# Binary cross entropy on one core: how the rows of the second chunk and of the last two stores are dealt to the 16 DMA engines

## The chip, the core and the metric

One core of a Trainium2 chip. The metric is the device time of one execution in microseconds (us). Before the change three runs gave 1864.62, 1865.15 and 1865.41; the median is 1865.15 us.

## The reference

Two float32 arrays of 8192 x 8192 go in, one comes out; target holds 0 or 1.

```python
pred = np.clip(pred, 1e-7, 1 - 1e-7)
return -(target * np.log(pred) + (1 - target) * np.log(1 - pred))
```

Since target is 0 or 1, the result is -ln|target - 1 + pred|, and so the kernel computes it: clip, add target - 1, absolute value, logarithm, times -1.

## The kernel before, in words

**Tiling.** The arrays are taken as flat; 64 Mi elements over 128 partitions are 524288 columns. `plan` (lines 17 to 24) cuts them into chunks: two of `FIRST` = 5120 columns, 35 of `BIG` = 14336, two of `LAST` = 5632 and one of `TAIL` = 1024. A chunk is one contiguous stretch of memory, cut into 128 rows, a row for each partition; a row of a `FIRST` chunk is 20480 bytes, of a `BIG` one 57344, of a `LAST` one 22528, of the `TAIL` one 4096.

**Buffers.** `ring_p` holds prediction chunks in three slots of `BIG` columns and a place for the tail; everything is computed in place there and stored from there. `ring_t` holds one target chunk as bf16; the transfer that loads it converts. The first two chunks share a slot.

**Queues.** Transfers are issued from three queues. ScalarE (ACT) issues the first prediction load as two halves (lines 69 and 70). GpSimd (POOL) issues all other loads (lines 72 and 75) and most stores (line 79). SyncE (SP) issues the stores of the last three chunks (a and b by line 79, c by `store_rows`, line 84). All of them run on the same 16 DMA engines. `store_rows` cuts the last store into 108, 12 and 8 rows. A transfer of fewer than 128 rows need not use all 16 engines: the semaphore records show 12, 12 and 8 landings for these three pieces, where one of 128 rows has 16.

**Compute.** VectorE (DVE) clips (`clip`, line 88), adds target - 1 (`log`, line 94) and multiplies by -1 (`back`, line 102); ScalarE does Abs and Ln between these (lines 97 and 98).

**Order.** It is written out by hand from line 104 on. At the start: both target loads and prediction loads of chunks 0 and 1, then the load of chunk 2; compute on 0 and 1; then the third target load (line 115), which may not be issued before line 94 of chunk 1 has read its target; then the stores of chunks 0 and 1 and the prediction load of chunk 3. In the middle, each chunk has its target load, its store and the prediction load two chunks on, in that order. At the end come chunks a, b (5632 columns each) and c (1024 columns).

Of the kernel before, what the change touches and what calls it, by code (L numbers as in the profile page):

```python
# [1 line left out]

# [4 lines left out]

EPS = 1e-7

BIG = 14 * 1024  # L10
FIRST = 5 * 1024
LAST = 5632
TAIL = 1024
SLOTS = 3


def plan(total):
    n = (total - 2 * FIRST - 2 * LAST - TAIL) // BIG
    assert n > 4 and total == 2 * FIRST + n * BIG + 2 * LAST + TAIL
    spots = [(FIRST, 0, 0), (FIRST, FIRST, FIRST)]  # L20
    spots += [(BIG, k % SLOTS * BIG, 0) for k in range(1, n + 1)]
    end = (n + 1) % SLOTS * BIG
    spots += [(LAST, end, 0), (LAST, end + LAST, LAST)]
    return spots + [(TAIL, SLOTS * BIG, BIG)]


@with_exitstack
def kernel(
    ctx: ExitStack,
    tc: tile.TileContext,  # L30
    pred: bass.AP,
    target: bass.AP,
    out: bass.AP,
):
    nc = tc.nc
    fp32 = mybir.dt.float32
    bf16 = mybir.dt.bfloat16
    Alu = mybir.AluOpType
    Act = mybir.ActivationFunctionType
    P = nc.NUM_PARTITIONS  # L40

    R, C = pred.shape
    spots = plan(R * C // P)
    n = len(spots)
    widths = [s[0] for s in spots]
    cols = [sum(widths[:k]) for k in range(n)]

    def chunk(ap, k):
        flat = ap.rearrange("r c -> (r c)")
        return flat[cols[k] * P : (cols[k] + widths[k]) * P].rearrange("(p w) -> p w", p=P)  # L50

    pool = ctx.enter_context(tc.tile_pool(name="rings", bufs=1))
    ring_p = pool.tile([P, SLOTS * BIG + TAIL], fp32, name="ring_p", tag="ring_p")
    ring_t = pool.tile([P, BIG + TAIL], bf16, name="ring_t", tag="ring_t")
    warm = pool.tile([1, 8], fp32, name="warm", tag="warm")

    def spot(k, part=(0, 1)):
        w, c, _ = spots[k]
        i, m = part
        return ring_p[:, c + i * w // m : c + (i + 1) * w // m]  # L60

    def spot_t(k, part=(0, 1)):
        w, _, c = spots[k]
        i, m = part
        return ring_t[:, c + i * w // m : c + (i + 1) * w // m]

    def load_p(k):
        if k == 0:
            for rows in (slice(0, P, 2), slice(1, P, 2)):
                nc.scalar.dma_start(out=spot(0)[rows], in_=chunk(pred, 0)[rows])  # L70
        else:
            nc.gpsimd.dma_start(out=spot(k), in_=chunk(pred, k))  # L72

    def load_t(k):
        nc.gpsimd.dma_start(out=spot_t(k), in_=chunk(target, k))  # L75

    def store(k):
        queue = nc.sync if k >= n - 3 else nc.gpsimd
        queue.dma_start(out=chunk(out, k), in_=spot(k))  # L79

    def store_rows(k):
        src, dst = spot(k), chunk(out, k)
        for first, last in ((0, 108), (108, 120), (120, 128)):
            nc.sync.dma_start(out=dst[first:last], in_=src[first:last])

    def clip(k, *part):
        p = spot(k, *part)
        nc.vector.tensor_scalar(  # L88
            out=p, in0=p, scalar1=EPS, scalar2=1 - EPS, op0=Alu.max, op1=Alu.min
        )  # L90

    def log(k, *part):
        p = spot(k, *part)
        nc.vector.scalar_tensor_tensor(  # L94
            out=p, in0=spot_t(k, *part), scalar=1.0, in1=p, op0=Alu.subtract, op1=Alu.add
        )
        nc.scalar.activation(out=p, in_=p, func=Act.Abs)  # L97
        nc.scalar.activation(out=p, in_=p, func=Act.Ln)  # L98

    def back(k, *part):  # L100
        p = spot(k, *part)
        nc.vector.tensor_scalar(out=p, in0=p, scalar1=-1.0, scalar2=None, op0=Alu.mult)  # L102

    with tc.manual_schedule():
        nc.vector.memset(warm, 1.0)  # L105
        load_t(0)
        load_p(0)
        load_t(1)
        load_p(1)
        load_p(2)  # L110
        nc.scalar.activation(out=warm, in_=warm, func=Act.Ln)  # L111
        for k in (0, 1):
            clip(k)
            log(k)
        load_t(2)
        back(0)
        store(0)
        back(1)
        store(1)
        load_p(3)  # L120
        a, b, c = range(n - 3, n)
        for k in range(2, n - 3):
            for h in (0, 1):
                clip(k, (h, 2))
                log(k, (h, 2))
            if k < n - 4:
                load_t(k + 1)
            else:
                load_t(a)
                load_t(b)  # L130
                load_p(c)
                load_t(c)
                back(k, (0, 2))
                for j in (a, b):
                    clip(j)
            if k < n - 4:
                back(k, (0, 2))
            back(k, (1, 2))
            store(k)
            if k + 2 < n - 3:  # L140
                load_p(k + 2)
            elif k + 2 == n - 3:
                load_p(a)
                load_p(b)
        log(a, (0, 2))
        log(a, (1, 2))
        clip(c)
        log(b, (0, 2))
        back(a, (0, 2))
        log(b, (1, 2))  # L150
        back(a, (1, 2))
        store(a)
        log(c)
        back(b, (0, 2))
        back(b, (1, 2))
        store(b)
        back(c)
        store_rows(c)


# [1 line left out]
_INS = ['pred', 'target']  # L162
_OUTS = [((8192, 8192), 'float32')]


# [23 lines left out]
```

## Time and profile before

| | |
|---|---|
| span of the profiled execution (first to last instruction) | 1863.3 us |
| runs, median of 3 | 1865.15 us (1864.62 to 1865.41) |
| DVE busy | 1121.6 us (60%) |
| ACT busy | 902.4 us (48%) |
| POOL busy | 178.7 us (10%) |
| prediction loads of 7168 KB, issue to landing, median | 44.3 us |
| target loads of 3584 KB, issue to landing, median | 31.3 us |
| stores of 7168 KB, issue to landing, median | 31.1 us |

The page gives the profiled execution's time as its span alone; the runs' median is 1.85 us more, for what lies ahead of the first instruction and behind the last.

How to read it: the DMA row has the mean busy share of the 16 engines in 40 slices of the span, in tenths. A stretch has the busy time of each compute engine, the granted TensorE clock (not used here), the DMA share and GB/s; a packet is counted where it starts, so a short stretch can show over 1.00. The GB/s count a target at the two bytes an element that are written, not the four that are read. In the order of time, a line has the start, the duration, the engine, the line of the program, the operation and its shape, how many, and in brackets how long the engine sat idle before it and what ended that. Beside these views the trace holds a record for each DMA packet (start, duration, size, queue, but not the engine) and one for each semaphore update (so, for each transfer, a landing for every engine that it used).

### The profile page before, as it was taken

To read this page: it belongs to the slowest core of one execution; us is meant where nothing else is said; L and a number is where in the kernel's file an instruction comes from. 1 tells how busy PE (TensorE), PEld (TensorE's weight loads), DVE (VectorE), ACT (ScalarE), POOL (GpSimd) and SP (SyncE) were. 2 spreads that over 40 slices of the span, in tenths; PEclk is the share of its full clock that TensorE was granted. 3 is DMA by queue.
4 is the path that set the end of the run, shared out by engine and by line. 5 is a ranking of instruction groups with operands and counts; after the bars stand their busy time and mean duration, and the time that the engine had idled before them with its cause. 6 is when DMAs were issued, how large, how long until landed. Compare 5 with 4: busy or idle time off the path is not lost.

```text
span 1863.3 us, 713 instructions
## 1 busy us (share of the span) xinstructions
DVE 1121.6 (60%) x230; ACT 902.4 (48%) x156; POOL 178.7 (10%) x120
## 2 busy tenths in 40 slices
DVE  4666555555666566655555666566655555666565
ACT  4454444455555544444445555544444445555554
POOL 1111101111110011101111110011101111110020
DMA  9999999999999999999999999999999999999999
GB/s 344 348 370 356 355 356 355 355 355 355 357 375 374 374 372 355 355 355 355 355 355 355 359 374 374 375 375 361 355 355 356 356 356 355 356 367 374 374 353 352
DMA packets 17318, 671.15 MB, mean 360 GB/s; under 512 B 1952, under 2 KB 1952, under 8 KB 2336
## 3 DMA queue, kind: packets, MB, share of 16 engines
q0 software_dynamic: 16704, 662.18, 99.0%
q1 hardware_dynamic: 448, 6.29, 0.8%
q10 hardware_dynamic: 160, 2.62, 0.4%
q14 instruction: 6, 0.05, 0.0%
HBM read 536.87 MB, written 268.44 MB: 432 GB/s over the span
## 4 chain that ended last, share of the span: by engine, by line
DMA 60%; issue 35%; ACT 3%; DVE 1%; POOL 0%; POOLq 0%; DVEq 0%; PEldq 0%
DMA ring_t<-in_target_dram 58%; DMA ring_p<-in_pred_dram 2%; ACT ring_p L98 1%; ACT ring_p L97 1%; DVE ring_p L94 1%; DVE ring_p L102 0%; POOL out_dram L79 0%; DVE ring_p L88 0%; POOL ring_t L75 0%; POOLq L75 0%; POOL ring_p L72 0%; POOLq L79 0%; DVEq L94 0%; PEldq L184 0%
## 5 line engine op out<-in xcount | busy, mean ns | idle before, releaser
L97 ACT ACTIVATE ring_p<-ring_p 128x7168 f32<-128x7168 f32 (+3 forms) x77 | 452.0, 5870 | 940.7 <-DVE ring_p L94 940.7
L94 DVE SCALAR_TENSOR_TENSOR ring_p<-ring_t,ring_p 128x7168 f32<-128x7168 bf16 (+3 forms) x77 | 558.2, 7251 | 372.0 <-DMA ring_t<-in_target_dram 370.7
L102 DVE TENSOR_SCALAR ring_p<-ring_p 128x7168 f32<-128x7168 f32 (+3 forms) x77 | 285.4, 3707 | 329.4 <-ACT ring_p L98 329.4
L98 ACT ACTIVATE ring_p<-ring_p 128x7168 f32<-128x7168 f32 (+3 forms) x77 | 452.6, 5877 | 2.4
L88 DVE TENSOR_SCALAR ring_p<-ring_p 128x7168 f32<-128x7168 f32 (+3 forms) x75 | 284.6, 3794 | 24.4 <-DMA ring_p<-in_pred_dram 24.4
L79 POOL DMA_DIRECT2D out_dram<-ring_p x37 | 128.0, 3459 | 584.4 <-DVE ring_p L102 584.2
L75 POOL DMA_DIRECT2D ring_t<-in_target_dram x40 | 29.0, 724 | 1057.2 <-DVE ring_p L94 1056.4
L72 POOL DMA_DIRECT2D ring_p<-in_pred_dram x39 | 21.8, 561 | 2.5 <-issue 2.5
L111 ACT ACT_TABLE_LOAD x1 | 1.3, 1283 | 1.9 <-issue 1.9
L105 DVE MEMSET warm<- 1x8 f32 x1 | 0.1, 65 | 0.8 <-PEq L173 0.8
L111 ACT ACTIVATE warm<-warm 1x8 f32<-1x8 f32 x1 | 0.2, 208 | 0.0
L173 POOL MEMSET const-float32-0.0<- 128x1 f32 x1 | 0.1, 99 | 0.2 <-issue 0.2
L173 POOL MEMSET const-bfloat16-1.0<- 128x1 bf16 x1 | 0.1, 102 | 0.0
L173 POOL MEMSET const-uint8-127<- 128x1 uint8 x1 | 0.1, 100 | 0.0
L173 POOL MEMSET const-float32-1.0<- 128x1 f32 x1 | 0.1, 99 | 0.0
## 6 DMA issues: line engine op xcount, KB each, us to landing
ring_p<-in_pred_dram POOLq DMA_DIRECT2D x35, 7168.0 KB, 44.3
out_dram<-ring_p POOLq DMA_DIRECT2D x35, 7168.0 KB, 31.1
ring_t<-in_target_dram POOLq DMA_DIRECT2D x35, 3584.0 KB, 31.3
ring_p<-in_pred_dram POOLq DMA_DIRECT2D x2, 2816.0 KB, 37.1
out_dram<-ring_p SPq DMA_DIRECT2D x2, 2816.0 KB, 14.6
out_dram<-ring_p POOLq DMA_DIRECT2D x2, 2560.0 KB, 27.9
ring_t<-in_target_dram POOLq DMA_DIRECT2D x2, 1408.0 KB, 26.5
ring_p<-in_pred_dram ACTq DMA_DIRECT2D x2, 1280.0 KB, 10.5
```

Source lines behind the costliest of these rows:

```text
L72: nc.gpsimd.dma_start(out=spot(k), in_=chunk(pred, k))
L75: nc.gpsimd.dma_start(out=spot_t(k), in_=chunk(target, k))
L79: queue.dma_start(out=chunk(out, k), in_=spot(k))
L88: nc.vector.tensor_scalar(out=p, in0=p, scalar1=EPS, scalar2=1 - EPS, op0=Alu.max, op1=Alu.min)
L94: nc.vector.scalar_tensor_tensor(out=p, in0=spot_t(k, *part), scalar=1.0, in1=p, op0=Alu.subtract, op1=Alu.add)
L97: nc.scalar.activation(out=p, in_=p, func=Act.Abs)
L98: nc.scalar.activation(out=p, in_=p, func=Act.Ln)
L102: nc.vector.tensor_scalar(out=p, in0=p, scalar1=-1.0, scalar2=None, op0=Alu.mult)
L105: nc.vector.memset(warm, 1.0)
L111: nc.scalar.activation(out=warm, in_=warm, func=Act.Ln)
L173: nc = _bacc.Bacc("TRN2", target_bir_lowering=False, num_devices=1)
```

## The change

The first two chunks become 4096 and 6144 columns. The second chunk's prediction load becomes five transfers: 112 rows; a small read of 8 rows x 16 elements into a new tile `turn` that nothing reads; 8 rows; the small read again; the last 8 rows. The small reads are there to move on the choice of engines, so that the eights fall to engines 8 to 15. The store of chunk b becomes three transfers of 112, 8 and 8 rows, and that of chunk c 48, 72 and 8 rows instead of 108, 12 and 8. What is computed stays the same.

```diff
-FIRST = 5 * 1024
+FIRST = 4 * 1024
+SECOND = 6 * 1024
...
-    n = (total - 2 * FIRST - 2 * LAST - TAIL) // BIG
-    assert n > 4 and total == 2 * FIRST + n * BIG + 2 * LAST + TAIL
-    spots = [(FIRST, 0, 0), (FIRST, FIRST, FIRST)]
+    n = (total - FIRST - SECOND - 2 * LAST - TAIL) // BIG
+    assert n > 4 and total == FIRST + SECOND + n * BIG + 2 * LAST + TAIL
+    spots = [(FIRST, 0, 0), (SECOND, FIRST, FIRST)]
...
+    turn = pool.tile([8, 32], fp32, name="turn", tag="turn")
...
         if k == 0:
             for rows in (slice(0, P, 2), slice(1, P, 2)):
                 nc.scalar.dma_start(out=spot(0)[rows], in_=chunk(pred, 0)[rows])
+        elif k == 1:
+            src, dst = chunk(pred, 1), spot(1)
+            nc.gpsimd.dma_start(out=dst[:112], in_=src[:112])
+            for i in range(2):
+                rows, few = slice(112 + 8 * i, 120 + 8 * i), slice(16 * i, 16 * i + 16)
+                nc.gpsimd.dma_start(out=turn[:, few], in_=src[:8, few])
+                nc.gpsimd.dma_start(out=dst[rows], in_=src[rows])
         else:
             nc.gpsimd.dma_start(out=spot(k), in_=chunk(pred, k))
...
-    def store_rows(k):
+    def store_rows(k, *ends):
         src, dst = spot(k), chunk(out, k)
-        for first, last in ((0, 108), (108, 120), (120, 128)):
+        for first, last in zip((0, *ends), (*ends, P)):
             nc.sync.dma_start(out=dst[first:last], in_=src[first:last])
...
-        store(b)
+        store_rows(b, 112, 120)
         back(c)
-        store_rows(c)
+        store_rows(c, 48, 120)
```

## The prediction

> **What bounds the kernel now.** I read the page first, then stretches of the span, then the order of time at both ends, then SyncE's waits.
>
> ```profile
> span 1863.3 us, 713 instructions
> ...
> DVE 1121.6 (60%) x230; ACT 902.4 (48%) x156; POOL 178.7 (10%) x120
> ...
> DMA  9999999999999999999999999999999999999999
> ...
> q0 software_dynamic: 16704, 662.18, 99.0%
> q1 hardware_dynamic: 448, 6.29, 0.8%
> ```
>
> No slice of the DMA engines is under 90%, while the busiest compute engine has 40% free. One chunk in the middle, and the last microseconds, as stretches:
>
> ```profile
> 1094.10:1144.84 50.74, 30.64 (x6) 24.60 (x5) 4.68 (x4) 1.00 1.00 362
> ...
> 1859.00:1860.00 1.00, 0.00 (x0) 0.00 (x0) 0.00 (x0) 1.00 0.96 352
> 1860.00:1861.00 1.00, 0.00 (x0) 0.00 (x0) 0.00 (x0) 1.00 0.22 88
> 1861.00:1862.00 1.00, 0.00 (x0) 0.00 (x0) 0.00 (x0) 1.00 0.08 33
> ```
>
> The last number but one is the DMA share: 1.00 in the middle. A chunk of 14336 columns moves 14336 x 128 x 12 bytes (prediction, target as read, output) in 50.74 us, 434 GB/s; the whole problem at that rate is 1855.5 us of the 1863.3. So the end is set by the transfers, and compute can cost only where it lets an engine's queue run dry. From 1860 on the share falls to 0.22 and 0.08: a few engines are still writing while the others are done. That tail is what the change addresses. SyncE shows who is waited for:
>
> ```profile
> SPq L184 <- DMA out_dram<-ring_p: 12.4, 3, 6.6
> ```
>
> The closing wait is for stores alone. Compute was over at 1848.14 (the last multiplication, line 102, starts at 1847.45 and takes 0.69), 10 us before the queue reached the last store.
>
> **Where each engine ends.** The semaphore records of the trace give a landing for each engine that a transfer used. The store of chunk b (16 landings) ends at 1858.32 to 1859.30 on eleven engines, 1860.05 on one, 1860.98 to 1861.31 on four. The three pieces of the last store have 12, 12 and 8 landings for 108, 12 and 8 rows. Matching them at one row's time apart: engines 0 to 7 (11 rows) end at 1860.12 to 1860.88, one at 1861.82; 8 to 11 (10 rows) at 1860.20 to 1860.60, one at 1862.31; 12 to 15 have none and end with b, which I take to be the late four, 1860.98 to 1861.31. The mean over 16 is 1860.8, so perfect levelling is worth 1.5 us, and 0.95 us of closing instructions follow whatever is last.
>
> **What the change does, engine by engine.** Row prices from the packet records: 20480 B in 761 ns, so a 24576 B row of the new second chunk 0.91 us; a 22528 B row of b 0.83; a 4096 B row of c 0.155. The first two prediction chunks hold the same bytes together. Intended rows:
> - Second chunk: 7 on engines 0 to 7, 9 on 8 to 15, instead of 8.
> - Store b: 112 rows are 7 each, the two eights go to 0 to 7: 9 and 7 instead of 8.
> - Store c: 48 rows are 3 each; 72 rows go to 12 engines, 6 each; 8 to 0 to 7: 10, 9 and 3 rows for 0 to 7, 8 to 11, 12 to 15, instead of 11, 10 and 0.
>
> That 72 rows take 12 engines I read from the landings: 108 and 12 rows used 12, 8 rows used 8, each the largest divisor up to 16. [...]
>
> The sum: 0 to 7: -0.91 + 0.83 - 0.155 = -0.23, plus the two 64-byte reads into `turn`; 8 to 11: +0.91 - 0.83 - 0.155 = -0.08; 12 to 15: +0.91 - 0.83 + 0.47 = +0.54. A 64-byte read isn't in the trace: between a 4 B packet (9 ns) and a 2048 B one (173 ns) each; I take 0.1 us for both, nearer the small one. So 0 to 7 gain 0.13.
>
> **What hides the rest.** POOL issues four more transfers at 0.54 us (first issues of lines 75 and 72): the third chunk's load is issued 2.2 us later, at 5.1 instead of 2.94, and is first needed when its forerunner ends near 27 us. SyncE issues two more stores (0.35 to 0.48 each): the last piece goes out near 1850 instead of 1849.1, needed from 1857.9. The smaller first chunk starts DVE earlier (it waited 14.2 us for it). DVE's clip of the second chunk waits for three landings instead of one; the last is the one that counts. That wait is the tight one:
>
> ```profile
> 28.65 2.83 DVE L88 TENSOR_SCALAR ring_p<-ring_p 128x5120 f32<-128x5120 f32 x1 [5.23 <-DMA ring_p<-in_pred_dram]
> 31.51 5.49 DVE L94 SCALAR_TENSOR_TENSOR ring_p<-ring_t,ring_p 128x5120 f32<-128x5120 bf16 x1
> 36.92 2.82 DVE L102 TENSOR_SCALAR ring_p<-ring_p 128x5120 f32<-128x5120 f32 x1
> 37.04 4.47 ACT L97 ACTIVATE ring_p<-ring_p 128x5120 f32<-128x5120 f32 x1 [4.61 <-DVE ring_p L94]
> 37.30 2.57 POOL L75 DMA_DIRECT2D ring_t<-in_target_dram  x1 [33.80 <-DVE ring_p L94]
> ```
>
> Line 75's load of the third target waits for the second chunk's line 94, and takes 2.57 us instead of 0.54: it ends just after DVE's line 102, beside which it runs. Now the second chunk lands 0.91 later (29.56), its clip takes 2.83 x 1.2 = 3.4 and line 94 5.49 x 1.2 = 6.6, ending at 39.6; line 102 on 4096 columns takes 2.3, so the load is issued by 42.0 instead of 39.87. Engines 0 to 7 finish the chunk before it (their packets end at 44.2 now) at 44.2 - 0.91 + 0.1 = 43.4. That leaves 1.4 us from issue to first packet. The rows that bound this delay: the first ACT load, issued at 0.74 with nothing ahead, has packets at 2.07 (1.3 us); the first POOL load, issued until 1.90, at 5.82, but behind four rows of the former (3.9 us). With 1.3, the nearer case, nothing runs dry; with 3.9 engines 0 to 7 idle 2.5 us. I take 0. Below nothing is excluded: an engine can't be more than busy. Later issues have 5 us and more of queue ahead. The eight-row store pieces and the 112-row load cost a 4 B packet each on an engine (9 ns): nothing.
>
> **A gain outside the ledger.** Where target rows end and store rows begin, the engines hold each other up. Two stretches of the DMA view, 58.9 to 60.1 and 105 to 107, with the last target row of every engine and nothing else:
>
> ```profile
> DMA packets 16, 0.46 MB, mean 382 GB/s; under 512 B 0, under 2 KB 0, under 8 KB 0
> ...
> q0 software_dynamic: 16, 0.46, 221.7%
> ...
> q0 software_dynamic: 16, 0.46, 113.1%
> ```
>
> 221.7% of 1.2 us is 2.66 us a row, 113.1% of 2.0 is 2.26, against 2.13 undisturbed: 0.53 and 0.13 lost on the mean engine. The late ones lose most: the spread of 16 landings is 0.96 us at 44.6, 1.60 at 61.8, 2.05 at 107.8, 2.40 at 158.5, 3.0 at 1858, and the four latest stay four. Once they are over 2 us behind, about one row, they lose 0.04 to 0.35 a chunk and then nearly nothing. All such excess after 20 us, summed over the packet records, is 20 us, 1.25 an engine. With the change 8 to 15 enter 1.8 us behind 0 to 7 before the first such place, by bytes rather than by loss. I estimate that they settle where the late four are now, 2.4 (8 to 11) to 2.8 (12 to 15) behind the leaders, and that the leaders, eight instead of twelve, lose 0.25 less. Then, from b's leaders at 1858.32 - 0.91 + 0.1 = 1857.5: engines 12 to 15 end at 1857.5 + 2.8 - 0.83 + 0.47 = 1859.9; 8 to 11 at 1857.5 + 2.4 - 0.83 + 9 x 0.155 = 1860.5; 0 to 7 at their former times less 0.13 and 0.25, the latest 1861.82 - 0.38 = 1861.44. That is 0.87 under 1862.31. The span is 1863.3, the runs' median 1865.15 (1864.62 to 1865.41); the page gives the execution's own time only as the span, and I carry the difference of 1.85 over: **1864.3**.
>
> **Rivals.**
> - The ledger alone (0.2): the losses come back on top of the skew. Latest: 8 to 11 at 1862.23, or, if the 4096 B packet of 1385 ns that made that one engine late doesn't recur, 12 to 15 at 1861.31 + 0.54 = 1861.85. Time 1864.7 to 1865.1. For it: the losses of the late four. Against: they stopped at a skew that the change gives.
> - Slower: the eight-row loads land on engines 0 to 7 (0.15), since nothing in the trace shows POOL transferring so few rows; the change doesn't do what it says. Then 0 to 7 carry 9 rows of the second chunk and 9 of b: +0.91 + 0.83 - 0.155 = +1.58, the latest at 1863.4, 1.1 later: 1866.2. It decides once it exceeds 0.49, the gap from 1861.82 to 1862.31. [...]
> - The third target load comes late (0.1): up to 2.5 us idle on 0 to 7, their latest at 1861.69 + 2.5 = 1864.2, 1.9 later: 1865.0 to 1867.0. It decides when the delay passes 1.4 us.
>
> **How the numbers follow.** The forecast has 0.45; 0.1 is for what I don't see, half of it beyond 0.2%. The likeliest case's own range is 1863.4 to 1864.9. The range takes in the ledger and the eight-row rival, and on the low side the full levelling with half of the losses saved (1.5 + 0.6): 1863.0 to 1866.3. About 0.2% (3.7 us) is what a measurement of this kernel tells from no change. Levelling (1.5) and all losses (1.25) together are less than that, so faster by over 0.2% has 0.02; slower needs two rivals at once or something unseen, 0.03; within, 0.95.
>
> **What would show it.** Right: the spread of the third target's landings grows from 1.0 to about 2.7 us at 62 us; two groups of eight; the rows in the first two such stretches take nearer 2.13 us; the DMA share holds until 1861 and then falls at once. Wrong: a gap in the DMA share at 43 to 46 us (late load), a spread that shrinks at 30 us (rows on 0 to 7), or a last landing past 1862.3.

## The result, and the profile after

The changed kernel takes 1884.99 us (median of 4 runs, 1883.47 to 1886.73), the kernel before 1865.28 beside it (4 runs, 1864.62 to 1865.58): a ratio of 1.0106, interval 1.0094 to 1.0118. It is 19.7 us slower, where 1864.3 was forecast and 1866.3 was the upper end.

The page of the changed kernel, the lines that answer to those shown of before:

```profile
span 1883.2 us, 725 instructions
...
DVE 1121.5 (60%) x230; ACT 902.3 (48%) x156; POOL 180.3 (10%) x124
...
DMA  9999999999999999999999999999999999999998
GB/s 255 346 363 353 353 351 352 358 361 367 371 374 375 364 351 352 358 361 353 354 364 352 358 374 375 371 370 363 361 352 356 364 351 353 358 361 358 371 356 316
...
q0 software_dynamic: 16816, 662.71, 98.7%
q1 hardware_dynamic: 468, 6.29, 0.9%
```

Compute did the same work in the same time, the bytes are the same, and the DMA row still shows nearly no idle slice. A reader who stops there finds no cause. The GB/s row says more: its first and last slice are the lowest. Stretches at both ends of the changed kernel and one chunk in its middle (columns as in the prediction; the last two are the DMA share and GB/s):

```profile
20.00:30.00 10.00, 0.00 (x0) 5.68 (x2) 0.00 (x0) 1.00 1.12 273
30.00:40.00 10.00, 0.00 (x0) 0.00 (x0) 0.00 (x0) 1.00 0.95 160
40.00:50.00 10.00, 9.82 (x2) 0.00 (x0) 0.00 (x0) 1.00 1.06 459
...
1866.00:1870.00 4.00, 0.00 (x0) 0.00 (x0) 0.00 (x0) 1.00 1.02 393
1870.00:1874.00 4.00, 0.00 (x0) 0.00 (x0) 0.00 (x0) 1.00 0.63 197
1874.00:1878.00 4.00, 0.00 (x0) 0.00 (x0) 0.00 (x0) 1.00 0.35 97
1878.00:1882.50 4.50, 0.00 (x0) 0.00 (x0) 0.00 (x0) 1.00 0.07 27
...
1104.00:1154.74 50.74, 30.68 (x7) 24.63 (x5) 4.67 (x3) 1.00 1.00 362
```

And the kernel before at its start:

```profile
20.00:30.00 10.00, 4.77 (x2) 6.51 (x2) 0.00 (x0) 1.00 1.12 460
30.00:40.00 10.00, 9.71 (x3) 5.39 (x2) 2.57 (x1) 1.00 0.87 378
```

The middle is as before (362 GB/s, share 1.00). From 20 to 40 us the engines count as busy just as before (1.12 and 0.95 against 1.12 and 0.87) but move 273 and 160 GB/s instead of 460 and 378: they are **busy and slow**, not idle. That is also why the page's DMA row hides it.

Three landings place the loss. The third chunk's prediction first lands at 54.2 us instead of 44.6 (+9.6). The last target chunk of 14336 columns first lands at 1794.2 instead of 1781.9 (+12.3). The last store lands at 1881.9 instead of 1862.3 (+19.6). So about 9.6 us are lost at the start, 2.7 on the way, 7.3 in the tail.

The order of time at the start of the changed kernel, against the stall of 5.23 us that the prediction showed:

```profile
40.14 3.36 DVE L97 TENSOR_SCALAR ring_p<-ring_p 128x6144 f32<-128x6144 f32 x1 [21.73 <-DMA ring_p<-in_pred_dram]
43.54 6.56 DVE L103 SCALAR_TENSOR_TENSOR ring_p<-ring_t,ring_p 128x6144 f32<-128x6144 bf16 x1
50.01 2.29 DVE L111 TENSOR_SCALAR ring_p<-ring_p 128x4096 f32<-128x4096 f32 x1
50.13 5.32 ACT L106 ACTIVATE ring_p<-ring_p 128x6144 f32<-128x6144 f32 x1 [24.42 <-DVE ring_p L103]
50.40 2.02 POOL L84 DMA_DIRECT2D ring_t<-in_target_dram  x1 [44.90 <-DVE ring_p L103]
```

DVE waits 21.73 us, until 40.14, for the last of the three pieces. They land at 30.6 to 32.6 (112 rows), up to 36.6 (first eight) and up to 40.0 (second eight). The packet records say why. In the 112 rows, a 24576 B row takes mostly about 1.5 us (0.92 to 1.86) instead of 0.91. The two eights take 2.7 to 3.9 us a row, and the second eight starts, row for row, when the first ends (30.08 + 2.71 = 32.79, 30.13 + 2.81 = 32.94): both run on **the same eight engines**. The other eight engines have gone on to the third chunk meanwhile, and their first row of it takes 7.7 to 8.6 us; undisturbed it takes 2.1.

The tail, in SyncE's part of the trace of the changed kernel:

```profile
1852.86 0.40 SPq L88 DMA_DIRECT2D out_dram<-ring_p  x1
1860.30 13.72 SPq L93 DMA_DIRECT2D out_dram<-ring_p  x6
```

Six stores take 13.72 us to issue, where three of the kernel before took 1.31. Of b's 128 rows, 0.84 us each before, 32 take 0.9 to 3.5 us; the 96 others take at most 0.89. The first guess could be that SyncE is late; the experiments show otherwise.

### The profile page after: what moved, and what is told of

It is laid out like the page before. It is cut to its first block, busy times and chain, and to the rows that moved or that the text cites. A ratio compares the mean times of both kernels' runs of the same rounds, so it can differ in the third digit from the quotient of the medians.

```text
span 1883.2 us, 725 instructions
## 1 busy us (share of the span) xinstructions
DVE 1121.5 (60%) x230; ACT 902.3 (48%) x156; POOL 180.3 (10%) x124
## 4 chain that ended last, share of the span: by engine, by line
DMA 59%; issue 36%; ACT 2%; DVE 1%; POOL 0%; POOLq 0%; DVEq 0%; PEldq 0%
DMA ring_t<-in_target_dram 57%; DMA ring_p<-in_pred_dram 2%; ACT ring_p L107 1%; ACT ring_p L106 1%; DVE ring_p L103 1%; DVE ring_p L111 0%; POOL out_dram L88 0%; DVE ring_p L97 0%; POOL ring_t L84 0%; POOLq L84 0%; POOL ring_p L81 0%; POOLq L88 0%; DVEq L103 0%; PEldq L193 0%
```

## The experiments

**The theories.** The measured rows suggested one that the prediction didn't have: the price of a row depends on which SBUF partitions the rows that move at the same time lie on; engines that write (or read) neighbouring partitions share one way in, and whoever waits there holds up the others as well. Its rivals: it is the skew between two groups of engines that costs, wherever the rows lie; it is the small reads into `turn`; it is the chunk sizes; it is SyncE's slow issuing; it is transfers of less than 128 rows as such.

**Taking the change apart.** start_only has the change's start and the old tail. sizes_only has 4096 and 6144 columns in whole loads. b_only and c_only have the kernel before with one store cut anew:

```diff
 # b_only
-        store(b)
+        store_rows(b, 112, 120)
 # c_only
-        store_rows(c)
+        store_rows(c, 48, 120)
```

> The start of the change alone (4096 and 6144 columns, the second prediction load in 112 rows, small read, 8 rows, small read, 8 rows); both last stores as before. Theory A (a transfer whose rows lie on few neighbouring partitions makes several DMA engines work on the same place of SBUF, which slows them and holds up others): about +11 to +13 us against before, packets of 24576 B at 1.5 us in the 112-row load and 2.7 to 3.9 us in the eight-row ones, as in the profile after. If instead the loss of the start is given back later or belongs to the tail: under +3 us. The spread of landings in mid-run should reach about 3.7 us as in the profile after.

> Only the sizes 4096 and 6144, the second prediction load whole; both last stores as before. Theory A: within 1 us of before, rows of the 6144-column prediction at 0.91 us. Rival B (the larger second chunk itself: its longer rows load slowly, or the third target load comes too late for its queue): +8 to +12 us, rows of 24576 B at 1.5 us or a gap in the DMA share between 40 and 60 us.

> Before, with only the store of chunk b cut into 112, 8 and 8 rows. Theory A: +3 to +6 us: rows of 22528 B in these stores at 1.3 to 2.7 us, and the last landing is on an engine with many slow rows. Rival C (the tail's loss is SyncE's slow issues, 2.3 to 3.2 us each in the profile after instead of 0.35 to 0.48): the two eight-row stores are issued late, but the queue holds work until 1858, so under +2 us. If the issues take 0.4 us here, the slow issues come from something else than the cut of b.

> Before, with only the store of chunk c cut into 48, 72 and 8 rows instead of 108, 12 and 8. Theory A: little, within 1 us of before, since the 4096 B rows are short and 108 and 12 rows lay no better: 0 to 7 lose a row, 12 to 15 gain 3, so the end moves by -0.5 to +0.5 us. Rival C: issues of 2.4 us each if the piece count or the shape 48 or 72 is what slows SyncE; then up to +3 us.

| kernel | median us | above before, us | ratio and interval |
|---|---|---|---|
| start_only | 1879.8 | 15.1 | 1.0078 (1.0062 to 1.0093) |
| sizes_only | 1867.56 | 2.9 | 1.0021 (1.0012 to 1.003) |
| b_only | 1870.52 | 5.9 | 1.003 (1.0018 to 1.0041) |
| c_only | 1864.88 | 0.2 | 1.0001 (0.9992 to 1.001) |

15.1 + 5.9 + 0.2 is 21.2, against 19.7 for the whole: the parts add up nearly (start_only holds the sizes too). The new cut of c is free, as costed. The sizes cost 2.9 us at the median, where under 1 was expected, and their 11 runs spread from 1866.79 to 1874.84; start_only, too, is above the 11 to 13 expected of it. What costs most is the second chunk's load in pieces and the store of b in pieces. In b_only SyncE issues its stores in 0.34 to 0.55 us, but for one of 1.23, and the tail is nearly as slow (5.9 us of 7.3). Its stretches:

```profile
1850.00:1855.00 5.00, 0.00 (x0) 0.00 (x0) 0.00 (x0) 1.00 1.02 428
1855.00:1860.00 5.00, 0.00 (x0) 0.00 (x0) 0.00 (x0) 1.00 1.05 290
1860.00:1865.00 5.00, 0.00 (x0) 0.00 (x0) 0.00 (x0) 1.00 0.40 102
```

The kernel before in the same stretches, but that it ends at 1863:

```profile
1850.00:1855.00 5.00, 0.00 (x0) 0.00 (x0) 0.00 (x0) 1.00 1.01 433
1855.00:1860.00 5.00, 0.00 (x0) 0.00 (x0) 0.00 (x0) 1.00 0.93 387
1860.00:1863.00 3.00, 0.00 (x0) 0.00 (x0) 0.00 (x0) 1.00 0.10 40
```

From 1855 on the engines of b_only are fully busy at 290 GB/s where 387 was. Slow issuing isn't needed for the loss: it goes with the slow rows in the changed kernel and is nearly absent here. The slow rows in b_only are again 32 of b's 128 (0.9 to 3.9 us); the 96 others take 0.84 to 0.88. Only 16 rows are in the eights, so at least 80 rows of the 112-row piece ran at nearly full pace: a store cut at 112 isn't slowed as the load is, where nearly every row was.

**Eight rows at a time, on neighbours and apart.** near8 leaves the kernel before as it is and adds four loads of eight rows (20480 B each), behind the second chunk's load, to partitions 112 to 119 and 120 to 127; nothing uses them (`w1` is the second chunk's width). far8 sends the same rows to every fourth partition of 96 to 127:

```diff
+        if k == 1:
+            src = chunk(pred, 1)[112:120]
+            for i, rows in enumerate((slice(112, 120), slice(120, 128)) * 2):      # near8
+            for i, rows in enumerate((slice(96, 128, 4), slice(97, 128, 4)) * 2):  # far8
+                free = slice(2 * BIG + i // 2 * w1, 2 * BIG + (i // 2 + 1) * w1)
+                nc.gpsimd.dma_start(out=ring_p[rows, free], in_=src)
```

> Before, plus four extra loads of the same eight rows of memory (20480 B each) into a free part of ring_p, right behind the second chunk's whole load: to partitions 112 to 119, 120 to 127, and the same again beside them. The extra data are not used. Each DMA engine gets two rows more, undisturbed 1.5 us. Theory A (neighbouring partitions slow several engines at once): rows at about 3.2 us, as the 3.9 us of the 24576 B rows, so +5 to +8 us against before. Rival D (the slowness comes from the memory side, from the small transfer's size, or from its issue): near8 and far8 alike.

> As near8, with the same rows of memory, sizes and number of transfers, but to partitions 96, 100, ..., 124 and 97, 101, ..., 125. Theory A: rows near 0.8 us, +1 to +2.5 us against before. Rival D: as near8.

In the same way b is stored as rows 0 to 95 and four eights, of neighbours (b_near) or of every fourth partition (b_far):

```diff
-        store(b)
+        for rows in (slice(0, 96), slice(96, 104), slice(104, 112), slice(112, 120), slice(120, P)):  # b_near
+        for rows in (slice(0, 96), *(slice(96 + i, P, 4) for i in range(4))):                        # b_far
+            nc.sync.dma_start(out=chunk(out, b)[rows], in_=spot(b)[rows])
```

> Before, with the store of chunk b cut into rows 0 to 95 and four eights of neighbours (96 to 103, and so on). If the eights fall on engines 0 to 7, these have 10 rows of b and 8 to 15 have 6: undisturbed the latest of 0 to 7 ends 1.2 us later than now. Theory A: rows of 22528 B in the eights at 2 to 4 us, +8 to +12 us. Rival D2 (a store is slowed by the shorter list of engines alone): like b_far.

> As b_near, but the four eights take every fourth row of 96 to 127. Theory A: rows at 0.84 us, +0.5 to +2.5 us against before (the load of 10 rows on half of the engines stays). Rival D2: as b_near.

| kernel | median us | above before, us | ratio and interval |
|---|---|---|---|
| near8 | 1880.75 | 16.1 | 1.0085 (1.007 to 1.01) |
| far8 | 1873.42 | 8.8 | 1.0046 (1.0031 to 1.0061) |
| b_near | 1873.12 | 8.5 | 1.0046 (1.0031 to 1.0061) |
| b_far | 1870.2 | 5.6 | 1.0031 (1.0019 to 1.0042) |

The bytes, the number of transfers and the rows on each engine are the same in near8 and far8; only the partitions differ, and 7.3 us with them. The theory's order is right and its sizes aren't: near8 was expected at 5 to 8 us, far8 at 1 to 2.5. For far8 the packet records say why: after the first round its rows take 1.57 to 1.61 us, twice the undisturbed 0.761. That asked for a third place. In the stores b_near is 2.9 us above b_far, and its slowest row of b takes 4.3 us against 2.6; but b_far, expected at 0.5 to 2.5, is slow as well, and no run stored its eights from other partitions.

**The other half of SBUF.** low8 sends the eights to every fourth partition of 0 to 31, in place of 96 to 127:

```diff
+            for i, rows in enumerate((slice(0, 32, 4), slice(1, 32, 4)) * 2):
```

> As near8 and far8, the same rows of memory, but to partitions 0, 4, ..., 28 and 1, 5, ..., 29. In near8 and far8 all four eights ran one after the other on the same eight engines (near8: rows 3.3 us, far8: 1.6 us, undisturbed 0.76), while the other eight engines were held to the same pace in the third chunk's first row. Theory A2: two engines that write the same group of partitions share one way into SBUF; far8's partitions belong to the upper half, which the other eight engines were filling, so each way had two engines. If the eights run on the engines of the lower half (0 to 7), low8 has no sharing: rows 0.76 to 0.8 us, the other engines undisturbed (2.1 us), and +2 to +3.5 us in all for four rows (3.05 us) on one half of the engines. If they run on the upper half's engines, low8 is like far8 (+8 us, rows 1.6 us). Rival D3 (an eight-row transfer runs at half pace whatever the partitions, or the memory side slows it): like far8. [...]

low8 takes 1871.29 us, 6.2 above (1.0034, 1.0021 to 1.0047). The three traces in one and the same stretch, while the eights move; near8:

```profile
28.00:38.00 10.00, 7.07 (x2) 4.20 (x1) 0.00 (x0) 1.00 0.80 95
```

far8:

```profile
28.00:38.00 10.00, 8.39 (x3) 4.38 (x2) 0.00 (x0) 1.00 0.98 330
```

low8:

```profile
28.00:38.00 10.00, 9.34 (x3) 5.33 (x2) 0.72 (x1) 1.00 0.97 421
```

95, 330 and 421 GB/s for the same queue of work. (A packet counts where it starts, which is why near8, with packets of up to 9 us, shows a share of 0.80 here and 1.41 in the stretch of 20 to 30 us.) In packets:

| | a row of the eights (0.761 us undisturbed) | the other eight engines' first row of the third chunk (2.116 us) |
|---|---|---|
| near8, partitions 112 to 127 | 3.26 to 3.30 us after the first round: 4.3 times | 7.9 to 9.5 us: 3.8 to 4.5 times |
| far8, every fourth of 96 to 127 | 1.57 to 1.61 us after the first round: 2.1 times | 3.8 to 4.5 us: 1.8 to 2.1 times |
| low8, every fourth of 0 to 31 | 0.761 us: once | 2.116 us: once |

In all three the four rounds follow one another on the same eight engines (near8: 27.32, 28.91, 32.17, 35.46). So the few-row transfer isn't slow as such; the place of its rows makes it slow. And both columns rise by nearly the same factor: the other eight engines, which move other rows, are held to the pace of the eights. low8 has the same rows and transfers, so if the rest costs the same in all three, the place alone is worth what the two others take beyond it: 9.9 of near8's 16.1 us (its third chunk first lands 10.6 us late) and 2.6 of far8's 8.8 (3.3 late). The other 6.2 us are low8's own, where no row at the start is slow; 2 to 3.5 were expected. They are taken up below.

**What the three places say of the theory.** low8 went out with a sharper form of it, the supposition A2: engines that write the same group of partitions share one way in, and far8's eights met the other eight engines there. The order of the three places, 4.3 times, 2.1 times and once, is what A2 asks for. Which partitions form a group, which engine writes which, and how many engines met in one place, no run shows: no record names the engine of a packet. Nor does A2 say why eights on eight partitions at a time held up all eight other engines in near8 (7.9 to 9.5 us). So A2 stays the author's reading; what is measured is the price of a row at each place.

**Without eights at all.** By this reading a transfer of 64 rows on one half, if all 16 engines share it and it reaches half of the groups, should be twice as slow on each, and rows that reach both halves free, though both are cut in two. split112 loads the second chunk (5120 columns) as rows 0 to 111 and 112 to 127; halves64 as 0 to 63 and 64 to 127; b_evenodd stores b as even and odd rows:

```diff
 # split112: ((0, 112), (112, P)); halves64: ((0, 64), (64, P))
+        elif k == 1:
+            for rows in (slice(0, 64), slice(64, P)):
+                nc.gpsimd.dma_start(out=spot(1)[rows], in_=chunk(pred, 1)[rows])
 # b_evenodd
-        store(b)
+        for rows in (slice(0, P, 2), slice(1, P, 2)):
+            nc.sync.dma_start(out=chunk(out, b)[rows], in_=spot(b)[rows])
```

> Before, with the second chunk's prediction load cut into rows 0 to 111 and 112 to 127: no eight-row transfer, no small read. Theory A2: seven neighbouring rows an engine fall out of step with the groups; rows of 20480 B at about 1.25 us instead of 0.76 in the first part (as 1.5 for 0.91 in the profile after), and the 16 last rows, one an engine, on a quarter of one half: about 3 us each. +5 to +7 us against before. Rival E (only the eight-row transfers and the small reads cost): within 1 us of before.

> Before, with the second chunk's prediction load cut into rows 0 to 63 and 64 to 127. Theory A2, if rows are dealt in neighbouring fours to 16 engines: each part reaches half of the groups, so rows at about 1.5 us instead of 0.76, +4 to +7 us. If each part ran only on the engines of its own half, or cutting costs nothing: within 1 us of before.

> Before, with the store of chunk b cut into even and odd rows (two transfers of 64 rows over all partitions). Theory A2: every group is reached in each part, so rows stay near 0.84 us and the end moves by at most 1 us. Rival D2 (any cut of store b costs): +3 us and more, as b_only and b_far.

split112 takes 1872.12, 7.1 above (1.004, 1.0026 to 1.0054); halves64 1871.61, 6.5 above (1.0037, 1.0023 to 1.005); b_evenodd 1865.09, the same as before to 0.1 us (1.0, 0.9991 to 1.001). The start of halves64:

```profile
20.00:30.00 10.00, 3.22 (x1) 6.72 (x2) 0.00 (x0) 1.00 1.02 226
30.00:40.00 10.00, 4.95 (x2) 2.22 (x1) 0.00 (x0) 1.00 1.00 350
```

226 GB/s is about half of the 460 that the kernel before has there, at a full DMA share; a row takes mostly 1.55 to 1.61 us, twice 0.761. The third chunk's prediction first lands at 51.0 instead of 44.6: the 6.4 us at the start are the whole loss of 6.5. 128 rows on 16 engines are eight each; at 0.8 us more a row (1.55 to 1.61 against 0.761) that makes 6.4 us with all engines alike, an estimate that meets the measured loss. So neither skew nor few rows are needed for it. The same stretches of split112:

```profile
20.00:30.00 10.00, 3.45 (x1) 6.48 (x2) 0.00 (x0) 1.00 1.11 276
30.00:40.00 10.00, 5.08 (x2) 2.46 (x1) 0.00 (x0) 1.00 1.00 362
```

Its 112 rows take mostly about 1.3 us, the last 16 rows 1.6 to 2.9, and the third chunk first lands at 50.3. Why the rows of a 112-row piece are slower, no run shows: no record tells which rows an engine took. The tail of b_evenodd, beside b_only's 290 and 102:

```profile
1855.00:1860.00 5.00, 0.00 (x0) 0.00 (x0) 0.00 (x0) 1.00 0.97 413
1860.00:1865.00 5.00, 0.00 (x0) 0.00 (x0) 0.00 (x0) 1.00 0.12 48
```

Of its 128 rows of b one is slow (1.13 us). So a cut into even and odd rows is free in this store, and it isn't the cutting as such that costs. For a load there is no such run, but the first prediction load of the kernel before is cut in the same way, and from 5.3 us on its 20480 B rows take 0.76 to 0.77. That a part reaches every group doesn't by itself foretell this: it hangs on which engine takes which of the even rows, and no record shows that.

**The small reads, and the skew.** no_small is start_only without the two reads into `turn`. low8_two is low8 with two of its four eights, so that eight engines are two rows (1.5 us) behind instead of four:

```diff
 # no_small
-                nc.gpsimd.dma_start(out=turn[:, few], in_=src[:8, few])
 # low8_two
-            for i, rows in enumerate((slice(0, 32, 4), slice(1, 32, 4)) * 2):
+            for i, rows in enumerate((slice(0, 32, 4), slice(1, 32, 4))):
```

> The start of the change without the two small reads; both last stores as before (start_only with the small reads: 1879.8, +15.1 us). If the small reads don't move anything, the two eights follow each other on the same eight engines: +14 to +16 us, rows of 24576 B at 2.6 to 3.9 us in two rounds while the other eight engines sit in one row of 57344 B for 7 to 8.5 us. If without the small reads the eights alternate between the halves, each engine has 8 rows: the third chunk's first rows aren't held up by 8 us on one half, the landings show no two groups, and the time is 3 us or more away from start_only.

> low8 with two of the four eights: two rows of 20480 B more on engines 0 to 7, 1.52 us, without sharing (rows 0.76 us). By the sum of rows alone, the latest of 0 to 7 end at 1861.82 + 1.52 = 1863.3 instead of 1862.3: +1.0 us. If, as the prediction had it, a skew of that size ends the losses where target rows end: 0 to +1 us, and the excess of packets after 20 us stays under the 20 us of before. If a skew makes more of them, as low8 suggests (74 us in all, 62 after 20 us): +2 to +4 us.

no_small takes 1879.81, 14.9 above (1.008, 1.0066 to 1.0094), like start_only's 15.1. Its eights take 2.5 to 3.9 us in two rounds on the same eight engines, the other eight's first row 7.7 to 8.5: the small reads change neither the time nor the place. They don't turn the choice of engines; and a choice that moved on by eight engines with each transfer would have put no_small's two eights on different ones.

low8_two takes 1869.2, 4.3 above (1867.62 to 1871.7 in 8 runs; 1.0026, 1.0015 to 1.0036). No row is slow at the start. By the sum of rows alone, the latest end of engines 0 to 7, 1861.82 before by the prediction's matching, moves, if the eights run on these, to 1863.3 with two rows more and to 1864.9 with four: 1.0 and 2.6 us behind the 1862.31 that ends the kernel before. Against that stand 4.3 and 6.2. In low8's trace the landings of the third chunk come in two groups of eight about 3 us apart, and later target rows (28672 B) lose time where they meet the store rows: their excess over the undisturbed duration, summed over the packet records, is 60.4 us on 16 engines (3.8 each) against 16.9 before; 26.5 in low8_two's profiled run, which was its fastest. So the kernels with a skew lose more than its bytes, and not just once: low8 loses about 0.8 us on every engine at 258 us and about 1 at 412. Why there, the traces don't show; and the loss varies from run to run (no_small's profiled run, its slowest, has 100.9 us of it, start_only's 59.9).

## Why the prediction was wrong, point by point

**What held.** The end is set by the transfers; compute costs nothing; the middle of the run is as before, and c's new cut (0.2 us) costs nothing that can be measured. The third target load goes out at 50.40 and the third chunk's rows end from 53.7 on, so that rival stayed out. Of the prediction's signs of being wrong one came, a last landing past 1862.3 (1881.9); there is no gap in the DMA share from 40 to 50 us (1.06). The small reads, too, are as cheap as foreseen: 0.01 to 0.09 us a packet.

**The step that failed: the row prices.** "Row prices from the packet records: 20480 B in 761 ns, so a 24576 B row of the new second chunk 0.91 us; a 22528 B row of b 0.83." Those records are of transfers of 128 rows (or of even and odd halves), which spread over all of SBUF. In the new pieces the same rows take about 1.5 us (112 rows of the load), 2.7 to 3.9 (its eights) and 0.9 to 3.5 (a quarter of b). For eights on neighbours near8 shows the step by itself, and its opposite, low8, has the prices as written. The prediction bounded queues, issues and landings from both sides, but never asked whether a row's duration holds for other partitions. A second term, the new sizes, stood at nothing, since the bytes of the two chunks together are the same; sizes_only costs 2.9 us.

**"The eight-row store pieces and the 112-row load cost a 4 B packet each": failed by the same.** split112 alone costs 7.1 us, b_only 5.9, though most of b's 112 rows keep their price.

**Where the eights go: nearer the rival, whose price was wrong.** The forecast put both eights of the second chunk on engines 8 to 15, "7 on engines 0 to 7, 9 on 8 to 15", by a choice of engines that the small reads move on. No run shows such a choice: with the small reads and without them (no_small, two rounds of 2.5 to 3.9 us) both eights run on the same eight engines. That speaks for the rival with 0.15, which had them all on engines 0 to 7; which eight they are, no record names. In the stores the number of engines came out as costed (16, 12 and 8 landings for the 48, 72 and 8 rows of c, 16, 8 and 8 for the three pieces of b), but that the eights of b and c run on engines 0 to 7 no run shows either; what the trace has in place of that term's 0.83 us a row are 32 rows of b at 0.9 to 3.5. And the rival used the same undisturbed prices: 1866.2, not 1885. What the eights would have taken on the other eight engines isn't known: in every load here their rounds followed one another on the same eight.

**"A gain outside the ledger": failed.** It took the engines to lose "nearly nothing" once they are over 2 us behind. The landings of the third target are indeed in two groups, spread over 2.9 us, as foreseen (2.7). But low8 enters with such a spread and goes on losing, and the changed kernel's excess on target rows is 51.2 us over 16 engines, 3.2 each, where 16.9 was before. The spread at which the late four had settled was no sign that a spread is free.

**How the sum would have come out.** start_only is 15.1: the sizes 2.9; the rest, 12.2, is the 112-row piece, the eights and what the skew loses later. start_only's trace puts 9.3 of the 15.1 before 54 us: its third chunk first lands at 53.9 instead of 44.6. Two eights on neighbours would be 8 as half of near8's 16.1, an estimate that no run tests. The tail adds 5.9 for b and 0.2 for c. The pieces can't be added more finely, since they overlap: the 112 rows' tail runs beside the first eight.

**What stays open.** It is open why sizes_only costs 2.9 us: its rows aren't slow, but the first place where target rows meet store rows loses 16.3 us over 16 engines instead of 8.5, and the landings of its stores of a and b are spread over 3.7 and 4.2 us instead of 3.0. It is open why spread-out engines keep losing there, which is over half of low8's 6.2 us, and why the 112 rows of a store slow down less than those of a load. And it is open by what the engines with other partitions are held up: the pace is measured (near8's 7.9 to 9.5 us), the mechanism isn't.

No variant beat the kernel before; b_evenodd and c_only equal it.

## What to carry to other kernels

A transfer's row had no price of its own here (20480 B took 0.761, 1.6 or 3.3 us by place): before you cut a transfer, list which partitions its pieces touch and how many engines will be on them at once, and cut through all of SBUF (even and odd rows, free in the store tried here: 1865.09 us against 1865.06) rather than into blocks (64 and 64 rows: 6.5 us; 112 and 16: 7.1 us; four eights on neighbours: 16.1, of which 6.2 stay when no row is slow). Read the DMA share together with GB/s: in the changed kernel a share of 0.95 at 160 GB/s, where 0.87 at 378 was, stood for rows that took up to 3.9 us instead of 0.91 and 8.6 instead of 2.1. And when the most that levelling could bring is 1.5 us, one unpriced shape in the change outweighs it.

## What the runs showed of the hardware

- Eight engines writing to eight neighbouring partitions move 50 GB/s in all (8 x 20480 B in 3.29 us; in the changed kernel 8 x 24576 B in 3.9 us), against 26.9 GB/s for a single undisturbed engine (20480 B in 0.761 us). The 50 are the eights alone; each of the other eight engines moved 6 to 7 GB/s beside them (57344 B in 7.9 to 9.5 us).
- The other eight engines fall to nearly the same pace as the crowded ones: 57344 B rows of 2.1 us took 7.9 to 9.5 (near8) and 3.8 to 4.5 (far8).
- Two pieces of 64 rows, each on one half of the partitions, run at about half the rate at a full DMA share (halves64, 20 to 30 us: 226 GB/s instead of 460 at a share of 1.02; mostly 1.55 to 1.61 us a row instead of 0.761).
- In the changed kernel five issues on SyncE in a row take 2.3 to 3.3 us each, against 0.35 to 0.48 before. Slow rows alone don't bring this about: b_only has them too, with issues of 0.34 to 0.55 us but for one of 1.23, and b_evenodd, with one slow row, has an issue of 1.82. What the slow issues cost by themselves wasn't measured.
